# Moving the transposed activations onto multiples of 512 bytes in each partition

## The chip, the cores and the metric

The kernel runs on one core of one Trainium2 chip. The metric is the device time of one execution in microseconds (us); less is better. A run's figure is the median of several executions.

## The reference

Two layers of a decoder trunk over 256 tokens with a model width of 1024, all in float32. Per layer:

```
h = h + 0.5 * SwiGLU_a(RMSNorm(h))
u = RMSNorm(h);  z = u @ W_in          # three groups of columns, one per token mixer
y_A, y_B, y_C = MLA(z_A), DiffAttn(z_B), StickBreak(z_C)
g = sigmoid(u @ W_gate)
h = h + (g_A*(y_A W_oA) + g_B*(y_B W_oB) + g_C*(y_C W_oC)) @ W_out
h = h + 0.5 * SwiGLU_b(RMSNorm(h))
h = h + sigmoid(RMSNorm(h) @ W_pg) * (p[i] @ W_pe)
out = RMSNorm(h)                       # after the last layer
```

SwiGLU has 2816 hidden columns. Nearly all the work is products of the 256 token rows with weight matrices.

## The kernel before, in words

**Products in three parts.** Every weight tile (512 KB, 128 partitions of 1024 numbers) is loaded by SyncE's queue into `raw`; ScalarE rounds it into `whi` (L82) and VectorE puts what is left into `wlo` (L83). Activations are split in the same way into a high and a low part. A product is then three TensorE instructions of the helper `mm3`: high times high (L92), high activations times low weights (L93), low activations times high weights (L94), summed in one PSUM bank. In `mm3(o, lhs, rhs, ...)` the first operand is loaded into the array (the weight load, stationary), the second streams through it. Each of the three instructions has a load of its own.

**What is loaded.** The token block is the stationary operand nearly everywhere: 128 activations x 128 tokens, 512 bytes in each partition. The weights stream, mostly 512 columns at a time. The one exception is `qk_proj`, where the weights are loaded and the activations stream, 256 columns in two pieces of 512 bytes.

**Where the activations lie.** `xhi` and `xlo` hold the normalised, transposed activations, `[P, TB, KT, P]`: two blocks of tokens, eight pieces of the width, 128 tokens, which is 8192 bytes in a partition. `x_at(tb, kt)` picks one piece of 512 bytes. They feed the upward products of all four FFNs (`up`), the projections of the mixers (`v_proj`, `gates`, `mla_down`, `qk_proj`), the product with W_out (`half`) and the gate of the layer's end (`part` in `ple`). Other products take their stationary operand from other tiles: the downward products of the FFNs from `fhi`, `flo`; the output projections of the mixers from `yA`, `yB`, `yC`; MLA's upward projections from `cqT`, `ckT`; the product with W_pe from `pT`.

**Order.** An FFN goes through 11 chunks of 256 hidden columns. Chunk c gives 48 products with x (`up`: two token blocks, eight pieces, three parts), four transposes of the chunk before (`turn`), and 24 products with the `fhi`, `flo` of the chunk two before (`down`). In the mixer, products of `gates`, `qk_proj` and `v_proj` are fillers between the steps of the attention heads (`pipeline`). The tile framework puts the instructions of each engine in order and sets the semaphores.

**Places in a partition.** The pool `cp` (one buffer each) takes its tiles one after another in the order of the calls: `xhi`, `xlo`, `h0`, `h1`, `gcol`, `ones`, `nones` and so on. In the program that is compiled for the kernel before, the bytes at which the tiles start in each partition are:

| tile | first byte | past a multiple of 512 |
|---|---|---|
| `xhi`, `xlo` | 16512, 24704 | 128 |
| `h0`, `h1`, `gcol` | 32896, 36992, 41088 | 128 |
| `ones`, `nones` | 41344, 41856 | 384 |
| `whi`, `wlo`, `raw` | from 51200 on | 0 |
| `fhi`, `flo`, `yA`, `yB`, `yC`, `pT`, `cqT`, `ckT` | from 133632 on | 0 |

The first tile starts 128 bytes past a multiple because four small constants lie before it.

Of the kernel before, what the change touches and what calls it, by code (L numbers as in the profile page):

```python
# [8 lines left out]
F32 = mybir.dt.float32  # L9
# [5 lines left out]
P = 128  # L15
L = 2
# [8 lines left out]
NEG = -1.0e30  # L25
MLA_H, DIFF_H, SB_H = 8, 4, 8
ROPE_T = 10000.0
# ALiBi's slopes, powers of two: 1 / slope goes into q, the slope into the exponent's scale, both exactly
SLOPE = [2.0 ** (-8.0 * (j + 1) / DIFF_H) for j in range(DIFF_H)]
U = 1024  # L30

# [2 lines left out]
def trunk(ctx: ExitStack, tc: tile.TileContext, a: dict, out: bass.AP):  # L34
# [3 lines left out]
    cp = ctx.enter_context(tc.tile_pool(name="cp", bufs=1))  # L38
# [10 lines left out]
    def const(name, shape):  # L49
        t = cp.tile(shape, F32, tag=name, name=name)  # L50
        tc.keep_in_program_order(nc.sync.dma_start(t, a[name]))
        return t

    xhi = cp.tile([P, TB, KT, P], F32R, tag="xhi", name="xhi")
    xlo = cp.tile([P, TB, KT, P], F32R, tag="xlo", name="xlo")
    h = [cp.tile([P, D], F32, tag=f"h{tb}", name=f"h{tb}") for tb in range(TB)]
    A.preload_act_table_set("silu_and_others")
    gcol = const("gcol", [P, L, 4, KT])
    late = [
# [7 lines left out]
    mhalf = cp.tile([P, 1], F32, tag="mhalf", name="mhalf")  # L67
    G.memset(mhalf, -0.5)

# [1 line left out]
    def load(src, n=U, pool=None, step=U):  # L71
        raw = wp.tile([P, U], F32, tag="raw", name=nm("raw"), bufs=4)
        if pool is None:
# [9 lines left out]
            V.tensor_tensor(out=lo[:, c], in0=raw[:, c], in1=hi[:, c].bitcast(F32), op=ALU.subtract)  # L83
        return hi, lo

    # keeps an activation behind the load of its table
    def behind(ins, table):
        order = mybir.DependencyInfo(mybir.DependencyClass.NoSync, mybir.DependencyReason.DATA)
        tc.add_manual_dep(ins.ins, table.ins.name, order, reason="behind")
# [35 lines left out]
        A.copy(hi, t)  # L125
        V.tensor_tensor(out=lo, in0=t, in1=hi.bitcast(F32), op=ALU.subtract)  # L126

# [1 line left out]
    def split_g(src, hi, lo, g):  # L129
        A.activation(hi, src, AF.Copy, scale=g)  # L130
        V.scalar_tensor_tensor(
# [12 lines left out]
            V.tensor_tensor(out=x4, in0=t.rearrange("p (j t) -> p j t", j=4), in1=gb, op=ALU.mult)  # L144
            split_T(x4, xhi[:, tb, 4 * n : 4 * n + 4, :], xlo[:, tb, 4 * n : 4 * n + 4, :])

# [1 line left out]
    def norm_r(tb, cuts=(0, 512, D)):  # L148
        n = len(cuts) - 1
        ss = small("ss", n)  # L150
# [14 lines left out]
        G.tensor_tensor(out=rr, in0=m, in1=mhalf, op=ALU.pow)  # L165
        return rr

    # the second block's transposes wait until a few products of the first have been issued
    pend = []

    def settle():
        while pend:
            pend.pop()()

# [1 line left out]
    def ffn(li, w13, w2, r, g, first=False, aside=None):  # L176
        with tc.tile_pool(name=nm("fp"), bufs=3) as fp:
            if first:
# [80 lines left out]
            pend.append(lambda: norm_T(1, g))  # L259
            return ro  # L260

# [1 line left out]
    def mixer(li, r, g_next):  # L263
        with tc.tile_pool(name=nm("xp"), bufs=1) as xp, tc.tile_pool(name=nm("tp"), bufs=2) as tp:
            HALF = (slice(0, P), slice(P, 3 * P))
            TOK = (slice(0, P), slice(P, 2 * P))
            made = {}

            # 1/rms along the free axis, on every partition
            def make_rbc():  # L270
                rbc = xp.tile([P, S], F32, tag="rbc", name=nm("rbc"))
                o = bank_tr()
# [4 lines left out]
                A.copy(rbc, o[:, :S])  # L277
                made["rbc"] = rbc

            # differential lambda, and the gains of its sub-norm  # L280
            def make_lam():
                dots = small("dots", 2)
                j64 = sp.tile([P, 64], F32, tag="j64", name=nm("j64"), bufs=2)
# [11 lines left out]
                V.tensor_scalar_mul(gs, gsub[:, li : li + 1], 1.0 - lam_init)  # L295
                made["lam"], made["gs"] = lam, gs

# [1 line left out]
            def qk_proj(base, name):  # L299
                t = made[name] = xp.tile([P, 8, S], F32, tag="w0" if base else "w2", name=nm(name))  # L300
                for i in range(8):
# [22 lines left out]
                    A.mul(v[:, tb, :], o, r[tb])  # L324
                    yield 2

            # the gates' logits; their sigmoids follow together, with one change of the engine's table
            def gates(b):
                if b == 2:
                    gl = xp.tile([P, 2, TB, 512], F32, tag="w1", name=nm("gate"))  # L330
# [17 lines left out]
                    gt = made["gate", b, n]  # L348
                    behind(A.activation(gt, gt, AF.Sigmoid), made["table"])

            # merged += gate * (y W_o)
            def proj_o(b, name):
                y = made[name]
                squash(b)
# [31 lines left out]
                        xhi[:, tb, 4 * n : 4 * n + 4, :], xlo[:, tb, 4 * n : 4 * n + 4, :],  # L386
                    )

# [1 line left out]
            def mla_down():  # L390
                un = [load(a["wz"][li, i], 672) for i in range(KT)]
                cq2 = tp.tile([P, 2, 384], F32, tag="t2", name=nm("cq"), bufs=1)
# [83 lines left out]
                        else:  # L476
                            A.copy(fT[:, 4 * u : 4 * u + 4, TOK[tb]], src)

# [1 line left out]
            def scores(q, k):  # L480
                o = bank_acc()
                PE.matmul(o[:, 0:P], q[:, 0:P], k[:, 0:P], start=True, stop=True)
# [143 lines left out]
                        return  # L626
                    n -= k

            # one step of every head under way, the oldest first, then n units of filler
            def pipeline(heads, g, n):  # L630
                live, heads = [], list(heads)
                while live or heads:
# [65 lines left out]
            pend.append(lambda: norm_T(1, g_next))  # L698
            return ro

# [1 line left out]
    def ple_in(li, pool):  # L702
        pT = [pool.tile([P, 2, S], F32R, tag=f"pT{i}", name=nm("pT")) for i in range(2)]
        praw = pool.tile([P, 2, S], F32, tag="praw", name=nm("praw"))
# [4 lines left out]
    def ple(li, r, g_next, pT):  # L709
        last = g_next is None  # L710
        with tc.tile_pool(name=nm("pp"), bufs=1) as pp:
            tc.keep_in_program_order(A.preload_act_table_set("sigmoid_and_others"))
            pe = pp.tile([P, TB, D], F32, tag="pe", name=nm("pe"))
            un = [load(a["wpe"][li, j]) for j in range(2)]
            for tb in range(TB):
                for n in range(2):
                    o = bank_acc()
                    for kt in range(2):
                        w = [x[:, n * 512 : (n + 1) * 512] for x in un[kt]]
                        mm3(o, [x[:, kt, tb * P : (tb + 1) * P] for x in pT], w, kt == 0, kt == 1)  # L720
                    A.copy(pe[:, tb, n * 512 : (n + 1) * 512], o)
                    settle()

            def part(tb, n, c0, c1, un, hook=None):
                o = bank_mm()[:, : c1 - c0]
                for kt in range(KT):
                    w = [x[:, (kt % 2) * 512 + c0 : (kt % 2) * 512 + c1] for x in un[kt // 2]]
                    mm3(o, x_at(tb, kt), w, kt == 0, kt == KT - 1)
                    if hook is not None and kt == 4:
                        hook()  # L730
                sg = pp.tile([P, 512], F32, tag="sg", name=nm("sg"), bufs=2)[:, : c1 - c0]
                A.activation(sg, o, AF.Sigmoid, scale=r[tb])
                c = slice(n * 512 + c0, n * 512 + c1)
                V.tensor_tensor(out=sg, in0=sg, in1=pe[:, tb, c], op=ALU.mult)
                V.tensor_tensor(out=h[tb][:, c], in0=h[tb][:, c], in1=sg, op=ALU.add)

            if not last:
                ro = []
                for n in range(2):
                    un = [load(a["wpg"][li, n, j]) for j in range(4)]  # L740
                    for tb in range(TB):
                        part(tb, n, 0, 512, un, (lambda: norm_T(0, g_next)) if n and tb else None)
                        if n == 1:
                            ro.append(norm_r(tb))
                pend.append(lambda: norm_T(1, g_next))
                return ro

            # the last block, and the closing norm of each block of tokens
            gf = pp.tile([P, D], F32, tag="gf", name="gf")
            nc.scalar.dma_start(gf, a["gf"].to_broadcast([P, D]))  # L750
            uns = [[load(a["wpg"][li, n, j], pool=pp if n else None) for j in range(4)] for n in range(2)]
            for tb in range(TB):
                part(tb, 0, 0, 512, uns[0])
                o = pp.tile([P, D], F32, tag="of", name=nm("of"), bufs=2)
                hg = pp.tile([P, 512], F32, tag="hg", name=nm("hg"))
                V.tensor_tensor(out=hg, in0=h[tb][:, 0:512], in1=gf[:, 0:512], op=ALU.mult)
                if tb == 0:
                    part(tb, 1, 0, 512, uns[1])
                    rr = norm_r(tb)
                else:  # L760
                    part(tb, 1, 0, 256, uns[1])
                    part(tb, 1, 256, 512, uns[1])
                    rr = norm_r(tb, (0, 512, 768, D))
                A.mul(o[:, 0:512], hg, rr)
                nc.scalar.dma_start(out[tb * P : (tb + 1) * P, 0:512], o[:, 0:512])
                V.scalar_tensor_tensor(
                    out=o[:, 512:D], in0=h[tb][:, 512:D], scalar=rr, in1=gf[:, 512:D], op0=ALU.mult, op1=ALU.mult,
                )
                nc.sync.dma_start(out[tb * P : (tb + 1) * P, 512:D], o[:, 512:D])

    def start(pool):
        # keeps the tensor engine's clock up until the first products
        warm = bank_tr()
        for i in range(10):
            PE.matmul(warm[:, :P], ones, ones, start=i == 0, stop=i == 9)
        un, sq = [], []
        for k in range(0, KT, 2):
            t = pool.tile([P, 2, S], F32, tag="xraw", name=nm("xraw"), bufs=4)
            nc.sync.dma_start(t, a["xT"][:, k : k + 2, :])
            q = pool.tile([P, 2, S], F32, tag="xsq", name=nm("xsq"), bufs=4)  # L780
            for j in range(2):
                split_g(
                    t[:, j, :].rearrange("p (b t) -> p b t", b=TB), xhi[:, :, k + j, :], xlo[:, :, k + j, :],
                    gcol[:, 0, 0, k + j : k + j + 1],
                )
            un.append(load(a["w13a"][0, 0, k // 2], step=512))
            if k < KT - 2:
                A.activation(q, t, AF.Square)
            else:
                V.tensor_tensor(out=q, in0=t, in1=t, op=ALU.mult)  # L790
            sq.append(q)
        return sq, un

    # 1/rms of the first block's rows, from the transposed rows
    def start_r(sq):
        for t in sq[1:]:
            G.tensor_tensor(out=sq[0], in0=sq[0], in1=t, op=ALU.add)
# [22 lines left out]
    for li in range(L):  # L820
        g = [gcol[:, li, j, :] for j in range(4)]
# [6 lines left out]


def _layout(i):  # L830
    """The inputs laid out for the chip, and constants that depend on shapes alone."""
    import numpy as np

    f = {k: np.asarray(v) for k, v in i.items()}
# [4 lines left out]
    o["pT"] = c(f["p"].reshape(L, S, 2, P).transpose(0, 3, 2, 1))  # L839

    def tiles(w, kk, ncol):
        # [L, K, N] -> [L, N / ncol, K / (128 kk), 128, kk * ncol]
        l, k, n = w.shape
        w = w.reshape(l, k // (P * kk), kk, P, n // ncol, ncol)
        return c(w.transpose(0, 4, 1, 3, 2, 5).reshape(l, n // ncol, k // (P * kk), P, kk * ncol))
# [36 lines left out]
    q = np.arange(P)  # L882
# [27 lines left out]
```

## Time and profile before

| | us |
|---|---|
| median of 3 runs | 1370.15 (1369.04 to 1370.43) |
| span of the profiled execution | 1368.3 |
| TensorE busy in it | 1354.9, 6720 matmuls |
| VectorE, ScalarE busy | 815.5, 731.8 |

The profiler took one execution. Its record gives the span from its first to its last instruction; a device time of that same execution is not given beside it, and the median of the runs is 1.85 us above the span. The page that the profiler leaves has busy times per engine, the span in 40 slices, the chain of work that ended last, and groups of instructions by line and tile (`mm<-whi,xhi` is: into bank `mm`, `whi` streaming, `xhi` stationary). Further views list instructions in order of time. Matmuls overlap one another in the record (one of 512 columns is shown with some 390 ns), so what one product costs in a row of products is read from the starts: from one start to the next.

### The profile page before, as it was taken

The numbers are of one execution on the slowest core, as the hardware profiler recorded it, in microseconds if no ns is written. First come the engines' busy times: TensorE is split into PE (matmuls) and PEld (weight loads), VectorE is DVE, ScalarE is ACT, GpSimd is POOL, SyncE is SP. The second block draws the span as 40 slices with busy tenths as digits, with TensorE's granted clock in tenths as the row PEclk, the third lists the DMA queues.
The fourth block names the chain that finished last, engine by engine and source line by source line (L and its number), as shares of the span: only waits on it lengthen the run. The fifth ranks groups of instructions, "written<-read, shape, count | busy, mean of one in ns | idle before, by whom it ended". The sixth has DMA issues, their size and how long they took to land.

```text
span 1368.3 us, 17897 instructions
## 1 busy us (share of the span) xinstructions
PE 1354.9 (99%) x6720; PEld 1120.1 (82%) x6720; DVE 815.5 (60%) x1190; ACT 731.8 (53%) x1122; POOL 49.4 (4%) x110
## 2 busy tenths in 40 slices
PE   8999999999999999999999999999999999999997
PEld 6888889978778888888888888898788788888886
DVE  6655565666658655555765555665667676555555
ACT  5544456665775544444654444566667745444445
POOL 2000000001000000000100000000010000000000
PEclk9999999999999999999999999999999999999999
DMA  7855547534346565555555555473434464555542
GB/s 261 270 187 185 186 128 223 171 103 145 123 127 214 163 204 184 188 184 187 158 185 185 184 185 185 133 227 126 140 108 163 155 203 165 187 184 184 187 157 85
DMA packets 68342, 236.61 MB, mean 173 GB/s; under 512 B 8224, under 2 KB 8864, under 8 KB 68256
## 3 DMA queue, kind: packets, MB, share of 16 engines
q1 hardware_dynamic: 67824, 234.43, 53.0%
q8 instruction: 52, 0.85, 0.2%
q10 hardware_dynamic: 432, 1.05, 0.2%
q14 instruction: 34, 0.28, 0.1%
HBM read 234.40 MB, written 1.05 MB: 172 GB/s over the span
## 4 chain that ended last, share of the span: by engine, by line
PE 97%; ACT 1%; POOL 1%; DMA 1%; DVE 0%; SPq 0%; issue 0%; POOLq 0%; ACTq 0%
PE mm L92 22%; PE mm L94 21%; PE mm L93 21%; PE acc L92 8%; PE acc L94 8%; PE acc L93 8%; PE tr L213 1%; PE tr L140 1%; PE acc L516 1%; PE tr L509 1%; PE acc L602 1%; PE acc L483 1%; PE acc L584 1%; DMA xraw<-in_xT 1%; PE tr L472 1%; PE acc L540 0%
## 5 line engine op out<-in xcount | busy, mean ns | idle before, releaser
L83 DVE TENSOR_TENSOR wlo<-raw,whi 128x1024 fp32r<-128x1024 f32 (+3 forms) x450 | 535.5, 1200 | 280.8 <-ACT whi L82 274.6
L82 ACT CAST whi<-raw 128x1024 fp32r<-128x1024 f32 (+3 forms) x450 | 455.8, 1027 | 266.5 <-PE acc L94 133.3
L92 PE MATMUL mm<-whi,xhi 128*128 128x512 f32 (+1 forms) x1032 | 409.7, 398 | 1.8 <-ACT whi L82 1.8
L93 PE MATMUL mm<-wlo,xhi 128*128 128x512 f32 (+1 forms) x1032 | 407.1, 395 | 0.6 <-DVE wlo L83 0.6
L94 PE MATMUL mm<-whi,xlo 128*128 128x512 f32 (+1 forms) x1032 | 407.1, 395 | 0.0
L92 PEld LDWEIGHTS mm<-whi,xhi 128*128 128x128 f32 x1032 | 194.6, 189 | 47.5 <-ACT whi L82 2.4
L93 PEld LDWEIGHTS mm<-wlo,xhi 128*128 128x128 f32 x1032 | 195.0, 189 | 45.1 <-DVE wlo L83 2.1
L94 PEld LDWEIGHTS mm<-whi,xlo 128*128 128x128 f32 x1032 | 194.8, 189 | 45.4 <-DVE xlo L126 0.5
L92 PE MATMUL acc<-whi,fhi 128*128 128x512 f32 x352 | 141.1, 403 | 0.0
L200 ACT ACTIVATE act<-mm,r 128x256 f32<-128x256 f32 x88 | 41.8, 475 | 184.2 <-PE mm L94 184.0
L94 PE MATMUL acc<-whi,flo 128*128 128x512 f32 x352 | 137.1, 391 | 0.0
L93 PE MATMUL acc<-wlo,fhi 128*128 128x512 f32 x352 | 136.6, 390 | 0.0
L202 DVE SCALAR_TENSOR_TENSOR pr<-mm,r,act 128x256 f32<-128x256 f32 x88 | 42.3, 480 | 136.4 <-ACT act L200 136.4
L94 PEld LDWEIGHTS acc<-whi,flo 128*128 128x128 f32 x352 | 66.1, 188 | 14.8
L92 PEld LDWEIGHTS acc<-whi,fhi 128*128 128x128 f32 x352 | 66.2, 188 | 13.1 <-ACT fhi L125 1.1
L93 PEld LDWEIGHTS acc<-wlo,fhi 128*128 128x128 f32 x352 | 66.3, 188 | 12.3
L92 PE MATMUL mm<-xhi,whi 128*128 128x256 f32 x256 | 73.6, 288 | 0.0
L93 PE MATMUL mm<-xlo,whi 128*128 128x256 f32 x256 | 72.1, 282 | 0.0
L94 PE MATMUL mm<-xhi,wlo 128*128 128x256 f32 x256 | 72.1, 282 | 0.0
L92 PEld LDWEIGHTS mm<-xhi,whi 128*128 128x128 f32 x256 | 48.2, 188 | 2.0 <-issue 2.0
L93 PEld LDWEIGHTS mm<-xlo,whi 128*128 128x128 f32 x256 | 48.3, 188 | 0.0
L94 PEld LDWEIGHTS mm<-xhi,wlo 128*128 128x128 f32 x256 | 48.2, 188 | 0.0
(213 smaller groups left out, 1363.6 us busy)
## 6 DMA issues: line engine op xcount, KB each, us to landing
raw<-in_w13b SPq DMA_DIRECT2D x88, 512.0 KB, 4.5
raw<-in_w13a SPq DMA_DIRECT2D x84, 512.0 KB, 4.6
raw<-in_wg SPq DMA_DIRECT2D x48, 512.0 KB, 3.9
raw<-in_w2a SPq DMA_DIRECT2D x44, 512.0 KB, 4.2
raw<-in_w2b SPq DMA_DIRECT2D x44, 512.0 KB, 4.4
raw<-in_wqk SPq DMA_DIRECT2D x32, 512.0 KB, 4.3
raw<-in_wo SPq DMA_DIRECT2D x24, 512.0 KB, 4.5
raw<-in_wv SPq DMA_DIRECT2D x16, 512.0 KB, 4.3
```

Source lines behind the costliest of these rows:

```text
L82: A.copy(hi[:, c], raw[:, c])
L83: V.tensor_tensor(out=lo[:, c], in0=raw[:, c], in1=hi[:, c].bitcast(F32), op=ALU.subtract)
L92: PE.matmul(o, lhs[0], rhs[0], start=first, stop=False)
L93: PE.matmul(o, lhs[0], rhs[1], start=False, stop=False)
L94: PE.matmul(o, lhs[1], rhs[0], start=False, stop=last)
L140: PE.transpose(t[:, j * P : (j + 1) * P], h[tb][:, k * P : (k + 1) * P], ident)
L200: A.activation(act, o[:, :FC], AF.Silu, scale=r[tb])
L202: V.scalar_tensor_tensor(out=pr, in0=o[:, FC:], scalar=r[tb], in1=act, op0=ALU.mult, op1=ALU.mult)
L213: PE.transpose(t[:, j * S + tb * P : j * S + (tb + 1) * P], prs[tb][:, j * P : (j + 1) * P], ident)
L472: PE.transpose(t[:96, j * P : (j + 1) * P], f[:, 4 * u + j, :], ident)
L483: PE.matmul(o[:, P : 3 * P], q[:, P : 2 * P], k, start=True, stop=True)
L509: PE.transpose(t[:, j * P : (j + 1) * P], e[:, j * P : (j + 1) * P], ident)
```

## The change

Two tiles that nothing reads or writes are added to the pool `cp`: 96 floats (384 bytes) ahead of `xhi`, and 32 floats (128 bytes) behind `h`. Together they are 512 bytes. `xhi` and `xlo` then start at 16896 and 25088, which are multiples of 512; every tile behind the second pad moves by 512 bytes and so keeps its place modulo 512. As `h0` and `h1` stand between the pads, by the order of the calls they move by 384 bytes too, to 33280 and 37376. No instruction is added, removed or moved. The diff also empties the lines of comments and adds three lines, so that the lines behind it stand three later in the new file (`mm3`'s 92 to 94 become 95 to 97).

```diff
@@ -51,9 +51,12 @@
         tc.keep_in_program_order(nc.sync.dma_start(t, a[name]))
         return t
 
+
+    cp.tile([P, 96], F32, tag="pad", name="pad")
     xhi = cp.tile([P, TB, KT, P], F32R, tag="xhi", name="xhi")
     xlo = cp.tile([P, TB, KT, P], F32R, tag="xlo", name="xlo")
     h = [cp.tile([P, D], F32, tag=f"h{tb}", name=f"h{tb}") for tb in range(TB)]
+    cp.tile([P, 32], F32, tag="pad2", name="pad2")
     A.preload_act_table_set("silu_and_others")
     gcol = const("gcol", [P, L, 4, KT])
```

## The prediction

> **What bounds the kernel now.** I read the page's busy times first, then its clock row, then the chain that ended last.
>
> ```profile
> span 1368.3 us, 17897 instructions
> PE 1354.9 (99%) x6720; PEld 1120.1 (82%) x6720; DVE 815.5 (60%) x1190; ACT 731.8 (53%) x1122; POOL 49.4 (4%) x110
> ...
> PEclk9999999999999999999999999999999999999999
> ...
> PE 97%; ACT 1%; POOL 1%; DMA 1%; DVE 0%; SPq 0%; issue 0%; POOLq 0%; ACTq 0%
> ```
>
> TensorE is busy for 99% of the span, its clock is granted in full in every slice, and 97% of the chain that ended last is TensorE's. So the time is the number of products times what each adds to the row of products. The change leaves the number alone. It can act only by changing what one product costs. Next came the groups of instructions with their shapes kept apart, for the counts, and the waits of TensorE, for what else it stands still for.
>
> ```profile
> L92 PE MATMUL mm<-whi,xhi 128*128 128x512 f32 x1016 | 405.2, 399 | 1.8 <-ACT whi L82 1.8
> L92 PE MATMUL acc<-whi,xhi 128*128 128x512 f32 x64 | 25.5, 404 | 0.1
> L92 PE MATMUL mm<-xhi,whi 128*128 128x256 f32 x256 | 73.6, 288 | 0.0
> L93 PE MATMUL acc<-wlo,xhi 128*128 128x384 f32 x32 | 10.9, 339 | 0.0
> L93 PE MATMUL mm<-wlo,cqT 128*128 128x384 f32 x24 | 8.0, 335 | 0.0
> ```
>
> The loads of the stationary operand, from the same view:
>
> ```profile
> L92 PEld LDWEIGHTS mm<-whi,xhi 128*128 128x128 f32 x1032 | 194.6, 189 | 47.5 <-ACT whi L82 2.4 <-DVE sqk L309 0.7 <-issue 0.3
> L92 PEld LDWEIGHTS acc<-whi,fhi 128*128 128x128 f32 x352 | 66.2, 188 | 13.1 <-ACT fhi L125 1.1
> ```
>
> And the longest of TensorE's waits for another engine:
>
> ```profile
> PE tr L509 <- DVE e L546: 2.0, 2, 1.0
> ```
>
> Each product of a piece of x with a weight tile has three such instructions, L92 to L94, with equal counts. So 3 x (1016 + 64) = 3240 products of 512 columns load their stationary operand from `xhi` or `xlo`, 96 more have 384 columns, and 768 stream x instead. Waits for other engines are small: 2.0 us for VectorE and 1.8 us for ScalarE (the idle time in the first row) are the largest of the whole execution.
>
> The durations in these rows overlap, so they don't add up to time. The cost of a product is the distance between starts, and that is in the timeline of TensorE. The first two rows are the start of a run of 48 with x and of what follows it; the next two the same for a run of 23 with `fhi`, `flo`; the last two for a run of 48 with `yB`.
>
> ```profile
> 51.59 0.40 PE L92 MATMUL mm<-whi,xhi 128*128 128x512 f32 x1
> ...
> 62.75 0.60 PE L213 MATMUL tr<-ident,pr 128*128 128x128 f32 x4
> ...
> 63.42 0.40 PE L93 MATMUL acc<-wlo,fhi 128*128 128x512 f32 x1
> ...
> 68.65 0.40 PE L92 MATMUL mm<-whi,xhi 128*128 128x512 f32 x1
> ...
> 419.40 0.39 PE L92 MATMUL mm<-whi,yB 128*128 128x512 f32 x1
> ...
> 430.28 0.39 PE L92 MATMUL mm<-whi,yC 128*128 128x512 f32 x1
> ```
>
> With x: (62.75 - 51.59) / 48 = 232.5 ns. With f: 23 products from 63.42 to 68.65, 227.4 ns. With yB: 48 products from 419.40 to 430.28, 226.7 ns. Same 512 columns, same streaming tiles, same length of load (189 and 188 ns). What differs is the stationary tile. x starts 128 bytes past a multiple of 512 in its partition; f, y start on a multiple. The bank is no explanation: yB and x both go to `mm`. This is the change's comparison, made already inside the kernel before, and the main ground of the forecast. It is a correlation: x also lies lower in the partition than f and y, and its pieces follow each other at 512 bytes where those of f and y follow at 1024.
>
> An aligned tile isn't always fast, though. Behind an interruption of the row of products, aligned runs start slow and then settle. Again the first and last rows of stretches:
>
> ```profile
> 192.16 0.40 PE L92 MATMUL acc<-whi,fhi 128*128 128x512 f32 x1
> 193.55 0.40 PE L92 MATMUL acc<-whi,fhi 128*128 128x512 f32 x1
> 194.24 0.39 PE L92 MATMUL acc<-whi,fhi 128*128 128x512 f32 x1
> 196.74 0.39 PE L94 MATMUL acc<-whi,flo 128*128 128x512 f32 x1
> ...
> 243.88 0.34 PE L92 MATMUL mm<-whi,cqT 128*128 128x384 f32 x1
> 246.48 0.39 PE L92 MATMUL mm<-whi,ckT 128*128 128x512 f32 x1
> 249.25 0.49 PE L472 MATMUL tr<-ident,qf 128*96 128x128 f32 x3
> ```
>
> Six products from 192.16 take 231.7 ns each, eleven from 194.24 take 227.3; twelve with the aligned `ckT` take 230.8 and don't settle. The reader is to see two prices of an aligned product: about 231.2 unsettled, about 227.0 settled. x stays at its 232.5 over whole runs.
>
> **The change part by part.** *The pads.* No instruction writes or reads them; they take 512 bytes and no time. *h moves by 384 bytes too.* It is the stationary operand of transposes:
>
> ```profile
> L213 PEld LDWEIGHTS tr<-ident,pr 128*128 128x128 f32 x176 | 22.0, 140 | 5.7
> L140 PEld LDWEIGHTS tr<-ident,h 128*128 128x128 f32 x112 | 13.1, 140 | 2.7 <-DVE h L253 0.7
> ```
>
> `pr` lies on a multiple and h does not, and both loads take 140 ns: nothing gained. That also speaks a little against the forecast, since here the place of a loaded tile shows no price.
>
> *Upward products of the FFNs.* 4 FFNs x 11 chunks x 48 = 2112; the first chunk is left out because it starts up against its weights, so 2064. A run of them follows directly on a run with f, already settled in the rows above. Aligned, it should stay settled: 227.0, between f's 227.4 and yB's 226.7. 2064 x (232.5 - 227.0) = 11.4 us.
>
> *The other 1128 products of 512 columns.* They are the fillers and W_out, between heads and transposes, so they start after interruptions. I take ten unsettled products in a run of 48, as in the rows from 192.16 on: (10 x 231.2 + 38 x 227.0) / 48 = 227.9. 1128 x 4.6 = 5.2 us.
>
> *96 products of 384 columns.* The rows give 339 ns with x and 335 with `cqT`: 96 x 4 = 0.4 us.
>
> *256 columns.* The last stage and `qk_proj` have 48 + 768 such products; the last stage's run is
>
> ```profile
> 1354.85 0.28 PE L92 MATMUL mm<-whi,xhi 128*128 128x256 f32 x1
> 1360.42 0.28 PE L94 MATMUL mm<-whi,xlo 128*128 128x256 f32 x1
> ```
>
> 47 steps, 118.5 ns each. No aligned run of this width is in the trace. From yB's 226.7 at 512 and cqT's (246.48 - 243.88) / 15 = 173.3 at 384, a line gives 119.9 at 256: an estimate, 1.4 ns slower than now, or 816 x 1.4 = +1.1 us. The other end is the share that 512 columns gain, 2.4%: 2.8 ns, -2.3 us. I take nothing, the nearest row being on the line's side and close to it. The 96 products of 288 columns go with these, at nothing.
>
> *What becomes late next.* A chunk's other engines:
>
> ```profile
> 51.59:68.65 17.06, 17.06 (x77) 13.95 (x76) 9.97 (x10) 8.64 (x11) 0.00 (x0) 1.00 0.75 250
> ```
>
> In 17.06 us VectorE is busy 9.97, ScalarE 8.64, the DMA engines 75%. Shortened by 48 x 5.5 = 0.26 us the chunk still has room on all three. In the attention stages TensorE's two waits for VectorE (2.0 us together) lie behind fillers that shrink; a run of 48 fillers saves 0.22 to 0.27 us ahead of each, so I give 0.5 us back.
>
> *Sum:* 11.4 + 5.2 + 0.4 - 0.5 = 16.5 us. Against the profiled span that is 1368.3 - 16.5 = 1351.8; the median of the runs stands 1.85 us above that span, taken as unchanged: 1370.15 - 16.5 = 1353.7 us.
>
> [...]
>
> **The rivals.**
> *Place modulo 512 is not what slows x.* The cause is then what else sets x apart: low in the partition, or pieces 512 bytes apart. For it: h's loads against pr's above. Against it: `qk_proj` streams the same low tiles, and its 256 columns are not above the line through aligned widths as far as the last stage's row tells. The 3240 products stay at 232.5: 1370.2 us. [...]
> *The pads take no place*, because unused tiles are dropped. Then the program is the same: 1370.2 us.
> *Slower: aligned runs of x never settle.* The streaming weights, the loaded x and what ScalarE and VectorE write then all start on the same multiple, and an aligned run can be worse than x is now right behind an interruption:
>
> ```profile
> 411.40 0.40 PE L93 MATMUL mm<-wlo,yA 128*128 128x512 f32 x1
> 412.35 0.39 PE L94 MATMUL mm<-whi,yA 128*128 128x512 f32 x1
> ```
>
> Four steps in 0.95 us, 237.5 ns. Held over 2064 + 1128 = 3192 products it costs 3192 x 5.0 = 16 us: 1386 us. It decides from 3192 x 0.85 ns = 2.7 us on, that is where x's mean passes 233.4. Against it: yA's own run and the f run settle.
>
> **How the numbers follow.** The measurement of this kernel can't tell changes under 0.2% (2.7 us) from none. Aligned x at an aligned pace: 0.79, likeliest 1353.7. Its own bounds: at best every product at yB's 226.7 (3192 x 5.8 = 18.5), with 0.4 and 2.3, 21.2 us: 1349. At worst every product at the unsettled 231.2 (3192 x 1.3 = 4.1), less 0.5 and 1.1: 2.5 us, 1367.6. Place not the cause: 0.12. Pads without effect: 0.04. Slower: 0.05. The range is that of the first case, 1349 to 1368, and so leaves out the other 0.21. Faster 0.79, same 0.16, slower 0.05.
>
> **What would show it.** In the timeline after, a chunk's 48 products with x should take 10.9 us in place of 11.16, and chunks follow at 16.8 us in place of 17.06. The loads should keep 188 ns and the products of 256 columns 118 to 120 ns. If the chunk keeps 17.06, the place was not the cause. If x's runs start at 227 and climb, alignment was only part of it. If chunks shorten but the span doesn't, look for new waits of TensorE behind VectorE in the attention stages.

## The result

| | before | after |
|---|---|---|
| median of 4 runs, us | 1369.74 (1369.04 to 1370.43) | 1354.41 (1354.11 to 1354.78) |
| span of the profiled execution, us | 1368.3 | 1352.9 |
| its device time, us | | 1354.69 |

The ratio after to before is 0.9888 (95% interval 0.9874 to 0.9902): 15.3 us less by the medians, 15.4 by the spans. The instructions of every engine are the same and in the same order; only places in the partitions differ.

The page of the changed kernel, the same parts as shown of the kernel before:

```profile
span 1352.9 us, 17897 instructions
PE 1339.4 (99%) x6720; PEld 1118.3 (83%) x6720; DVE 815.5 (60%) x1190; ACT 731.6 (54%) x1122; POOL 49.3 (4%) x110
...
PEclk9999999999999999999999999999999999999999
...
PE 97%; ACT 1%; POOL 1%; DMA 1%; DVE 0%; SPq 0%; issue 0%; POOLq 0%; ACTq 0%
```

TensorE lost 15.5 us of busy time, VectorE none and ScalarE 0.2, and TensorE still makes 97% of the chain. So the products themselves became cheaper. The groups by shape (busy us, mean ns; `mm3`'s lines are now 95 to 97):

```profile
L95 PE MATMUL mm<-whi,xhi 128*128 128x512 f32 x1016 | 399.8, 394 | 1.8 <-ACT whi L85 1.8
L95 PE MATMUL mm<-xhi,whi 128*128 128x256 f32 x256 | 73.9, 288 | 0.0
L96 PE MATMUL acc<-wlo,xhi 128*128 128x384 f32 x32 | 10.8, 338 | 0.0
```

The largest of TensorE's waits (us in all, how often, the longest):

```profile
PE tr L512 <- DVE e L549: 2.1, 2, 1.0
```

The first of the three products of 512 columns with x went from 399 to 394 ns, those of 256 and 384 columns did not gain to speak of (288 and 288, 339 and 338 ns), and the largest wait of TensorE is 2.1 us in all, where it was 2.0. The timeline gives the cost of a product. The first two rows are the start of a run of 48 with x and of what follows, the next two the same for 23 with f, the last two the first and last of 48 with x at 256 columns:

```profile
84.66 0.39 PE L95 MATMUL mm<-whi,xhi 128*128 128x512 f32 x1
...
95.54 0.60 PE L216 MATMUL tr<-ident,pr 128*128 128x128 f32 x4
...
96.21 0.39 PE L96 MATMUL acc<-wlo,fhi 128*128 128x512 f32 x1
...
101.46 0.39 PE L95 MATMUL mm<-whi,xhi 128*128 128x512 f32 x1
...
1339.37 0.28 PE L95 MATMUL mm<-whi,xhi 128*128 128x256 f32 x1
...
1345.00 0.28 PE L97 MATMUL mm<-whi,xlo 128*128 128x256 f32 x1
```

With x a product takes (95.54 - 84.66) / 48 = 226.7 ns in place of 232.5. With f it is (101.46 - 96.21) / 23 = 228.3; all 36 such runs have a mean of 228.4 where the kernel before has 228.1. A chunk takes 101.46 - 84.66 = 16.80 us in place of 17.06. At 256 columns a product takes (1345.00 - 1339.37) / 47 = 119.8 ns in place of 118.5: dearer.

Adding up every distance from one product's start to the next, over the whole trace, after against before: products of 512 columns with x 16.5 us less, those of 256 columns 1.1 us more, every other kind within 0.2 us. Together that is the 15.4 us of the span.

### The profile page after: what moved, and what is told of

It reads as the page before. It is cut to its first block, busy times and chain, and to the rows that moved or that the text cites. A ratio compares the mean times of both kernels' runs of the same rounds, so it can differ in the third digit from the quotient of the medians.

```text
span 1352.9 us, 17897 instructions
## 1 busy us (share of the span) xinstructions
PE 1339.4 (99%) x6720; PEld 1118.3 (83%) x6720; DVE 815.5 (60%) x1190; ACT 731.6 (54%) x1122; POOL 49.3 (4%) x110
## 4 chain that ended last, share of the span: by engine, by line
PE 97%; ACT 1%; POOL 1%; DMA 1%; DVE 0%; SPq 0%; issue 0%; POOLq 0%; ACTq 0%
PE mm L95 22%; PE mm L97 21%; PE mm L96 21%; PE acc L95 8%; PE acc L97 8%; PE acc L96 8%; PE tr L216 1%; PE tr L143 1%; PE acc L519 1%; PE tr L512 1%; PE acc L605 1%; PE acc L587 1%; PE tr L475 1%; PE acc L486 1%; DMA xraw<-in_xT 1%; PE acc L543 0%
## 5 line engine op out<-in xcount | busy, mean ns | idle before, releaser
L95 PE MATMUL mm<-whi,xhi 128*128 128x512 f32 (+1 forms) x1032 | 404.3, 392 | 1.8 <-ACT whi L85 1.8
L96 PE MATMUL mm<-wlo,xhi 128*128 128x512 f32 (+1 forms) x1032 | 402.1, 390 | 0.6 <-DVE wlo L86 0.6
L97 PE MATMUL mm<-whi,xlo 128*128 128x512 f32 (+1 forms) x1032 | 402.3, 390 | 0.0
L95 PEld LDWEIGHTS mm<-whi,xhi 128*128 128x128 f32 x1032 | 194.0, 188 | 43.2 <-ACT whi L85 2.5
L96 PEld LDWEIGHTS mm<-wlo,xhi 128*128 128x128 f32 x1032 | 194.4, 188 | 40.8 <-DVE wlo L86 2.2
L97 PEld LDWEIGHTS mm<-whi,xlo 128*128 128x128 f32 x1032 | 194.2, 188 | 40.9 <-DVE xlo L129 0.9
L95 PE MATMUL acc<-whi,fhi 128*128 128x512 f32 x352 | 141.0, 402 | 0.0
L97 PE MATMUL acc<-whi,flo 128*128 128x512 f32 x352 | 137.2, 392 | 0.0
L96 PE MATMUL acc<-wlo,fhi 128*128 128x512 f32 x352 | 136.6, 390 | 0.0
L97 PEld LDWEIGHTS acc<-whi,flo 128*128 128x128 f32 x352 | 66.0, 188 | 14.7
L95 PEld LDWEIGHTS acc<-whi,fhi 128*128 128x128 f32 x352 | 66.2, 188 | 13.2 <-ACT fhi L128 1.1
L96 PEld LDWEIGHTS acc<-wlo,fhi 128*128 128x128 f32 x352 | 66.3, 188 | 12.7
L95 PE MATMUL mm<-xhi,whi 128*128 128x256 f32 x256 | 73.9, 288 | 0.0
L97 PE MATMUL mm<-xhi,wlo 128*128 128x256 f32 x256 | 72.4, 283 | 0.0
L96 PE MATMUL mm<-xlo,whi 128*128 128x256 f32 x256 | 72.4, 283 | 0.0
L95 PEld LDWEIGHTS mm<-xhi,whi 128*128 128x128 f32 x256 | 48.9, 191 | 2.0 <-issue 2.0
L96 PEld LDWEIGHTS mm<-xlo,whi 128*128 128x128 f32 x256 | 49.0, 191 | 0.0
L97 PEld LDWEIGHTS mm<-xhi,wlo 128*128 128x128 f32 x256 | 48.9, 191 | 0.0
```

The costliest lines, as they stand in the source:

```text
L95: PE.matmul(o, lhs[0], rhs[0], start=first, stop=False)
L96: PE.matmul(o, lhs[0], rhs[1], start=False, stop=False)
L97: PE.matmul(o, lhs[1], rhs[0], start=False, stop=last)
```

## The experiments

That the products with x are cheaper is settled by the result. Open was what makes them cheaper. The first theory was the prediction's: the loaded tile's own place modulo 512. Its rivals: the move of h or of everything else; a smaller modulus; the relation of the loaded tile's place to the streaming tile's; something else about x. The kernel before was run again beside each group of experiments, with medians of 1369.06 to 1369.80 us; the ratios below are against these.

**x back, h and the rest moved.** The first pad goes behind `xlo`.

```diff
-    cp.tile([P, 96], F32, tag="pad", name="pad")
     xhi = ...
     xlo = ...
+    cp.tile([P, 96], F32, tag="pad", name="pad")
     h = ...
```

> xhi and xlo back at 128 past a multiple of 512, h alone on a multiple, everything behind moved by the same 512 bytes as in the changed kernel. Theory (the place of a loaded tile modulo 512 sets the pace of the products that run beside the load): products of 512 columns with x at 232.5 ns again, time 1370 us. Rival (h's move, or the move of everything else by 512 bytes, made the gain): 1354.5 us.

Measured: 1369.55 us, ratio 1.0001 (0.9992 to 1.0011); the run of 48 with x from 86.17 to 97.33 us, 232.5 ns each. The place of x alone makes the gain; h's, and the shift of all else by 512 bytes, nothing.

**x at 256 past a multiple of 512.** The first pad is 128 bytes, another of 256 stands behind `xlo`.

> xhi and xlo 256 bytes past a multiple of 512, all else as in the changed kernel. Theory with modulus 512 (a load of 512 bytes must not cross a multiple of 512): 232 to 233 ns per product with x, 1370 us. Rival (a multiple of 256 is enough): 227 ns, 1354.5 us.

Measured: 1353.84 us, ratio 0.9892 (0.9875 to 0.9908).

```profile
83.62 0.39 PE L96 MATMUL mm<-whi,xhi 128*128 128x512 f32 x1
...
94.51 0.60 PE L217 MATMUL tr<-ident,pr 128*128 128x128 f32 x4
```

(94.51 - 83.62) / 48 = 226.9 ns. The modulus 512 fell: here every load of 512 bytes crosses a multiple of 512, and nothing is lost by it. For x, 256 past the multiple is as good as none.

**xlo alone off.** A pad of 128 bytes between `xhi` and `xlo`, the second pad left out.

> xhi on a multiple of 512, xlo (and h) 128 bytes past one. A third of the loads is off. Theory, price per load: 1080 products pay 5.0 to 5.5 ns, 1360 us. Rival, price per state (one off load in three keeps the whole run from settling at 227): nearly all of it back, 1366 to 1370 us.

Measured: 1364.59 us, ratio 0.9968 (0.9957 to 0.9980): 10 us above the changed kernel, two thirds of the gain lost for one off load in three, between the two expectations. The groups by shape show which products pay. First this run, then the same groups of the kernel before and of the changed one:

```profile
L97 PE MATMUL mm<-whi,xlo 128*128 128x512 f32 x1016 | 404.4, 398 | 0.0
L96 PE MATMUL mm<-wlo,xhi 128*128 128x512 f32 x1016 | 403.3, 397 | 0.8 <-DVE wlo L86 0.8
L95 PE MATMUL mm<-whi,xhi 128*128 128x512 f32 x1016 | 399.5, 394 | 1.6 <-ACT whi L85 1.1 <-DVE pr L205 0.4
```

```profile
L93 PE MATMUL mm<-wlo,xhi 128*128 128x512 f32 x1016 | 402.6, 397 | 0.6 <-DVE wlo L83 0.6
L94 PE MATMUL mm<-whi,xlo 128*128 128x512 f32 x1016 | 402.6, 396 | 0.0
```

```profile
L96 PE MATMUL mm<-wlo,xhi 128*128 128x512 f32 x1016 | 397.6, 392 | 0.6 <-DVE wlo L86 0.6
L97 PE MATMUL mm<-whi,xlo 128*128 128x512 f32 x1016 | 397.8, 392 | 0.0
```

The order is 95, 96, 97. L95 has the changed kernel's 394 ns; L96 and L97 have 397 and 398, about what they had before, and not the changed kernel's 392. From start to start the median step is 227 ns behind L95, 233 behind L96 and 234 behind L97. While L96 streams, `xlo` is being loaded (in the changed kernel's trace a product of L96 starts at 84.88 us and a load of `xlo` at 84.89); while L97 streams, the next `xhi` is (both start at 85.11). So in this run an off load costs the product beside it and the one after.

**The weights off, x on.** Pads of 128 and 384 bytes around `whi` and `wlo` (some small tiles shrunk to make room; `raw` and all tiles behind keep their places modulo 512).

```diff
...
+            if not shifted:
+                wp.tile([P, 32], F32, tag="padw", name="padw")
             hi = wp.tile([P, U], F32R, tag="whi", name=nm("whi"), bufs=7)
             lo = wp.tile([P, U], F32R, tag="wlo", name=nm("wlo"), bufs=7)
+            if not shifted:
+                shifted.append(wp.tile([P, 96], F32, tag="padw2", name="padw2"))
...
```

> x on a multiple of 512 as in the changed kernel, the weight tiles whi and wlo (streaming nearly everywhere, loaded in qk_proj alone) 128 bytes past one. Theory, the place of the loaded tile counts alone: products of 512 columns with x, f, y stay at 227 ns; 768 loads of weights are off, at 256 columns, where off loads showed no price (118.5 ns in the last stage before); 1354.5 us, at most 1358. Rival (loaded and streaming tile must start on the same place modulo 512): all 4700 products of 512 columns at 232, 1378 us.

Measured: 1376.70 us, ratio 1.0059 (1.0044 to 1.0074), slower than both kernels. Runs with x and with f in one chunk:

```profile
85.51 0.40 PE L101 MATMUL mm<-whi,xhi 128*128 128x512 f32 x1
...
96.72 0.60 PE L222 MATMUL tr<-ident,pr 128*128 128x128 f32 x4
...
97.38 0.39 PE L102 MATMUL acc<-wlo,fhi 128*128 128x512 f32 x1
...
102.74 0.40 PE L101 MATMUL mm<-whi,xhi 128*128 128x512 f32 x1
```

x: (96.72 - 85.51) / 48 = 233.5 ns; f: (102.74 - 97.38) / 23 = 233.0. Every loaded tile of these rows lies on a multiple of 512, and both kinds of product are slow. The time is close to the rival's 1378 us; the loaded tile's own place is not the cause.

One group in this run is an exception, and it says the same. In the last stage the weights for the second half of the columns come from another pool (`pool=pp`), and `load` adds the pads only where no pool is given. Their 24 products with x stand between two groups of 24 with moved weights; the rows are the first product of each group and of what follows:

```profile
1344.77 0.39 PE L101 MATMUL mm<-whi,xhi 128*128 128x512 f32 x1
...
1350.37 0.39 PE L101 MATMUL mm<-whi,xhi 128*128 128x512 f32 x1
...
1355.83 0.40 PE L101 MATMUL mm<-whi,xhi 128*128 128x512 f32 x1
...
1361.42 0.28 PE L101 MATMUL mm<-whi,xhi 128*128 128x256 f32 x1
```

The three groups take 233.3, 227.5 and 232.9 ns a product.

**Weights and x both at 128.** The same pads around the weights, and x as before the change.

> x 128 bytes past a multiple of 512 as in the kernel before, and whi, wlo 128 past one as well, so that loaded x and streaming weights share their place. Theory, the loaded tile's own place counts: x at 232.5 ns, f and y at 227, 1370 us. Rival (the two must share a place modulo 512): x at 227, and f, y, with their 1440 products, at 232: 1361 us.

Measured: 1359.67 us, ratio 0.9930 (0.9914 to 0.9947).

```profile
84.32 0.39 PE L101 MATMUL mm<-whi,xhi 128*128 128x512 f32 x1
...
95.20 0.60 PE L222 MATMUL tr<-ident,pr 128*128 128x128 f32 x4
...
95.88 0.39 PE L102 MATMUL acc<-wlo,fhi 128*128 128x512 f32 x1
...
101.21 0.39 PE L101 MATMUL mm<-whi,xhi 128*128 128x512 f32 x1
```

x: 10.88 / 48 = 226.7 ns, though x lies where it lay before the change. f: 5.33 / 23 = 231.7, though f was not moved. The last stage turns round too:

```profile
1327.82 0.40 PE L101 MATMUL mm<-whi,xhi 128*128 128x512 f32 x1
...
1333.29 0.40 PE L101 MATMUL mm<-whi,xhi 128*128 128x512 f32 x1
...
1338.88 0.39 PE L101 MATMUL mm<-whi,xhi 128*128 128x512 f32 x1
...
1344.34 0.28 PE L101 MATMUL mm<-whi,xhi 128*128 128x256 f32 x1
...
1349.97 0.29 PE L103 MATMUL mm<-whi,xlo 128*128 128x256 f32 x1
```

227.9 ns, then 232.9 with the weights that were not moved, then 227.5. With the run before, the four combinations are complete: fast where loaded and streaming tile share their place, slow where they are 128 bytes apart. The theory was changed to that, modulo 256.

**x at 64 past a multiple.** Pads of 448 and 64 bytes.

> xhi, xlo and h 64 bytes past a multiple of 512. Theory, any load that crosses a multiple of 512 pays the same: 232 to 233 ns, 1370 us. Rival (the price grows with the part of the load behind the multiple; 64 of 512 bytes is half of 128): 230 ns, 1362 us. Rival (a multiple of 64 is enough): 1354.5 us.

Measured: 1370.16 us, ratio 1.0004 (0.9995 to 1.0014). The run with x goes from 84.75 to 95.95 us, 233.3 ns each. Half the distance costs no less than 128 does.

**f off, x on.** Pads of 128 and 384 bytes around `fhi` and `flo` in the FFN's pool.

> x as in the changed kernel, fhi and flo (the FFNs' downward products) 128 bytes past a multiple of 512. Theory: their 1056 products go from 228 to 232.5 or 233 ns, and the runs of x behind them start unsettled: 1359 to 1361 us. Rival (something else of x, as its low place in the partition, made it slow): 1354.5 us.

Measured: 1358.34 us, ratio 0.9921 (0.9906 to 0.9936), 3.9 us above the changed kernel.

```profile
83.96 0.39 PE L95 MATMUL mm<-whi,xhi 128*128 128x512 f32 x1
...
94.84 0.60 PE L220 MATMUL tr<-ident,pr 128*128 128x128 f32 x4
...
95.51 0.39 PE L96 MATMUL acc<-wlo,fhi 128*128 128x512 f32 x1
...
100.87 0.40 PE L95 MATMUL mm<-whi,xhi 128*128 128x512 f32 x1
...
111.79 0.60 PE L220 MATMUL tr<-ident,pr 128*128 128x128 f32 x4
```

f went to 5.36 / 23 = 233.0 ns. So there is nothing special about x. The second half of the expectation, that the runs of x behind the off runs would start unsettled, came true in half the runs: the run from 83.96 keeps its 10.88 / 48 = 226.7, the next, from 100.87, takes (111.79 - 100.87) / 48 = 227.5, its first eight steps 231.4 on the mean. In the whole trace 16 of the 32 such runs start like the second. What kept the time under the expected 1359 to 1361 is f itself: from start to start its 1056 products take 4.0 us more than in the changed kernel, 3.8 ns each, where 4.5 to 5 had been expected.

**By order, without the two pads.** `gcol`, `mhalf`, `gmla` and `gsub` are put ahead of `xhi` and fill the gap of 384 bytes; `ones`, `nones`, `ident` and `eT` come onto a multiple too. For that a small tile of MLA goes to another pool, one scratch tile has one buffer in place of two, and a pad of 128 bytes stands in the pool of small tiles.

> No pads: four small tiles are put ahead of xhi and fill the gap; ones, nones, ident and eT, which lay off a multiple of 512, come to lie on one too, and the kernel takes 512 bytes less than the changed one. Theory: x as in the changed kernel, the others are too few to show, 1354.0 us, within 1 us. Rival (the slow starts behind transposes come from ident's and eT's place): some 700 products still above 228 ns settle too, 700 x 4.5 ns = 3 us less, 1351.5 us.

Measured: 1353.62 us, ratio 0.9886 (0.9871 to 0.9901). The rival's 1351.5 is not reached. Both versions were run once more side by side:

> The changed kernel once more, beside the version without pads on the same chip: 1354.4 us, within 0.7.

> The version without pads (small tiles first, all loaded and streaming operands on a multiple of 512) once more: theory, no difference from the changed kernel that can be told, 1353.5 to 1354.5 us. Rival (ident's and eT's place costs something): 0.7 us or more below the changed kernel of the same call.

Measured: 1353.84 us (1353.61 to 1354.08) and 1354.34 (1353.24 to 1354.38). No difference that can be told: the places of `ident` and `eT` show no price, and what makes the starts behind transposes slow is not shown. This version does without the pads around x and is as fast.

**x at 32 and at 192.**

> xhi, xlo (and h) 32 bytes past a multiple of 512, weights on one. Theory as it stands after the earlier runs (loaded and streaming tile must start on the same place modulo 256; any other distance is slow): products of 512 columns with x at 231 to 234 ns, 1368 to 1371 us. Rival (a small distance costs little, the price grows with the distance): below 229.5 ns, under 1362 us.

> xhi, xlo (and h) 192 bytes past a multiple of 512, weights on one. Theory (same place modulo 256 alone is fast): 231 to 234 ns, 1368 to 1371 us. Rival (places from 192 on are as good as 256): 227 ns, 1354.5 us.

Measured: 1369.80 us (ratio 1.0003, 0.9993 to 1.0012) and 1356.38 us (ratio 0.9906, 0.9891 to 0.9921). The runs of 48 with x, first of 32 (84.90 to 96.09), then of 192:

```profile
84.90 0.39 PE L95 MATMUL mm<-whi,xhi 128*128 128x512 f32 x1
...
96.09 0.60 PE L216 MATMUL tr<-ident,pr 128*128 128x128 f32 x4
```

```profile
84.78 0.39 PE L95 MATMUL mm<-whi,xhi 128*128 128x512 f32 x1
...
95.77 0.60 PE L216 MATMUL tr<-ident,pr 128*128 128x128 f32 x4
```

11.19 / 48 = 233.1 ns at 32, as expected. At 192 it is 10.99 / 48 = 229.0, which neither side had: "any other place is slow" is wrong too. By the distance of x behind the weights, modulo 256, a product of 512 columns costs:

| bytes | 0 | 32 | 64 | 128 | 192 |
|---|---|---|---|---|---|
| ns | 226.7 to 226.9 | 233.1 | 233.3 | 232.5 | 229.0 |

With the weights 128 bytes off in place of x it was 233.5; one FFN of that same run has 232.4, so 1 ns between two runs of products is no sign of a difference in places. Why 192 lies between, what happens from 192 to 256, and what in the chip makes the distance matter is open; no run here shows it.

## Why the prediction was right

Forecast were 1353.7 us, in a range of 1349 to 1368; measured were 1354.41.

*TensorE's products set the time.* Right: the whole difference is in distances between their starts.

*Upward products of the FFNs, 227.0 ns and 11.4 us.* Right. The 36 runs of 48 between transposes have a mean step of 227.0 ns (before 232.7); 32 of them, each behind a settled run with f, are settled from the first product on, at 226.7 to 226.8. The 2064 products gained 11.0 us.

*The other products of 512 columns, 227.9 ns and 5.2 us.* Right: without steps over 260 ns, which hold the interruptions, they have a mean of 227.6 ns, where the kernel before has 232.5. They gained 5.3 us. With 0.2 us from the first chunk, which the sum left out, the two terms measure 16.5 us, and 16.6 were forecast.

*384 columns, 0.4 us.* Wrong: nothing. The 192 products of 384 and 288 columns together take 29.8 us after and 29.9 before. The duration of single rows was no measure of the distance between starts.

*256 columns, nothing, with +1.1 us as one end.* Wrong, and that end came: the line through 512 and 384 columns gave 119.9 ns and 119.8 was measured; all 816 products cost 1.1 us more. The sum should have taken the estimate and not the row.

*0.5 us given back to waits.* Wrong: TensorE's waits for VectorE went from 2.0 to 2.1 us. With 0.4, 0.5 and 1.1 the three small terms are off by 1.0 us together, the two large ones by 0.1: 16.5 us were forecast against 15.4 in the span.

*The cause.* The forecast took the correlation inside the kernel before (x off, slow; f and y on, fast) as one of the loaded tile's own place modulo 512. That step is wrong in two parts: it is the distance between loaded and streaming tile, and 256 serves as well as 512. The time came out right all the same because the pads that put x on a multiple of 512 also put it at the weights' place. That was luck of the layout: with the weights at 128 the same reasoning was off by 22 us (1354.5 expected, 1376.7 measured). The trace of before could not tell these apart, since every streaming weight lay on a multiple of 512 there. The prediction named place low in the partition and pieces 512 bytes apart as confounders. The streaming tile's place, which was the one that counted, it named only in the rival that forecast a loss, as if sharing a multiple could do harm; here it is what helps.

*The rivals.* That place doesn't count fell with the result. With a load of x that is recorded at 189 ns before and 188 after, the running product takes 232.5 or 226.7 ns, as the two operands lie. The pads do take their place: 1354.41 us with both, 1369.55 with the first one behind `xlo`. Aligned runs of x do settle, 32 of 36 at 226.7 to 226.8 ns.

## What to carry to other kernels

Where every product loads a new stationary operand, look up where the loaded and the streaming operand start in a partition, and try the two at the same place modulo 256; in this kernel 0 and 256 bytes apart gave 226.7 and 226.9 ns, and 32 to 128 bytes apart cost 2.6 to 2.9% of each product of 512 columns. Moving both by the same 128 bytes is as good as aligning both for these products (226.7 ns), and moving the streaming tile away undoes what aligning the loaded one brings (233.5 ns). The price showed in no wait and no idle time (TensorE's largest wait was 2.0 us before and 2.1 after, the idle time ahead of the products with x 1.8 us in both); compare distances between starts of equal products whose operands come from different tiles, and check the sign for each width, since products of 256 columns went the other way, from 118.5 to 119.8 ns in the last stage.

## What the runs showed of the hardware that was not expected

The pace of a product of 512 columns followed the distance between the streaming operand and the one whose load is recorded beside it, 226.7 ns at 0 and 233.5 with the weights 128 bytes off, and not either one's own place: 226.7 too with both at 128. In the one run that tried it, one off load in three cost two products, with median steps of 233 and 234 ns. Products of 256 columns did otherwise: neither 128 nor 192 bytes was dearer than 0. With x at 192 the run of 48 that took 119.8 ns each after the change takes (1347.33 - 1341.80) / 47 = 117.7:

```profile
1341.80 0.28 PE L95 MATMUL mm<-whi,xhi 128*128 128x256 f32 x1
...
1347.33 0.28 PE L97 MATMUL mm<-whi,xlo 128*128 128x256 f32 x1
```

From start to start, the 768 products of `qk_proj` have a mean of 122.2 ns at 0, 120.9 at 128 and 118.3 at 192. But distance alone did not set the pace at this width: with weights and x both at 128, the last stage's narrow products have weights that were not moved, so they are as far from x as before the change, and they take (1349.97 - 1344.34) / 47 = 119.8 ns, not 118.5. Why is open. A version with the wide products at 0 and the narrow ones at 192 was not tried.
